# Hybrid decoder layer on one core: a third weight block loaded by halves into general buffers, and tiles at multiples of 128 bytes

## The chip, the cores and the metric

The kernel runs on one core of a Trainium2 chip. The metric is the device time of one execution in microseconds (us); less is better. Times of before are the median of three runs, and one further execution was taken with the hardware profiler on.

## What is computed

One layer with a residual stream of 256 tokens by 2048 channels. The input is normalised, multiplied by one wide matrix `w_in`, and split into the operands of two token mixers (a gated linear attention and a differential attention) and of two merge gates. Each mixer's output goes through its own 2048 by 2048 matrix, the two are merged, go through `w_out`, are normalised and added to the input.

```python
h = rmsnorm(x, pre_norm_g[l])
proj = h @ w_in[l]
(a_q, a_k, a_v, a_g, a_lr, b_q, b_k, b_v, b_g, m_a, m_b) = jnp.split(proj, offsets, axis=-1)
...
y_a = o_a @ w_branch_a[l]
...
y_b = o_b @ w_branch_b[l]
merged = jax.nn.sigmoid(m_a) * y_a + jax.nn.sigmoid(m_b) * y_b
out = merged @ w_out[l]
x = x + rmsnorm(out, post_norm_g[l])
```

## The kernel before

All weights are read once from memory, in 1 MB tiles of 128 by 2048 numbers, by DMAs that SyncE (SP in the profile) issues in a fixed order. Each tile is used as two halves of 128 by 1024. For a half, ScalarE (ACT) writes `hi`, the number rounded to the short format that the matrix unit takes at full rate (L231), and VectorE (DVE) writes `lo`, what the rounding left out (L232). TensorE (PE) then multiplies `hi` by the high and the low part of the activations and `lo` by the high part; the three products together keep the accuracy. `emit_half` prepares halves four ahead of their use (`AHEAD`), and `hi` and `lo` have three buffers each.

A matmul has two operands in on-chip memory (SBUF): a stationary one of 128 by 128, which a weight load (PEld) brings into the array, and a moving one of up to 512 columns, which streams past. Nearly every matmul here has a weight load of its own.

- In `half_tile` (L407) and `block_products` (L648) the activations are stationary and the weights move, 512 columns at a time. The activations are `xs` (the input), the pairs `oah`/`oal` and `obh`/`obl` (outputs of the two mixers), `mh`/`ml` (the merged stream), and `s4`, `r1`, `s2`, `r3` (sums of blocks of the input, from `sum_operands`).
- In `half_channel` (L427 with 512 columns, L429 with 256) the weights are stationary and `xs` moves.

The merge gate m_b is computed as two **sets**, `set0` and `set1`, by a block scheme with seven products in place of eight (`PRODUCTS`, in the order 1, 3, 5, 6, 2, 7, 4). A set's matrix is cut into four blocks, each of two tiles t = 0, 1. Blocks 1 and 4 are loaded by SP (`link`), the second block is added into the first by a DMA of GpSimd (POOL) that accumulates, and so on: the tiles `a` and `b` are changed in place from one product to the next. Product 2 uses the third block by itself (`raws[s, t]`, the tile `raw_c` in the profile), and `follow_set` then adds it into `a` on DVE (L186), a half at a time, for product 7. The steps of the two sets are interleaved with those of `others` (the last value group and the keys and queries of the first mixer), in the order that `phase_steps` writes out. In the profile this stage lies between about 81 and 277 us.

Where tiles lie is decided by pools. `const` comes first and holds tiles of odd sizes; then `wpool` (three buffers `raw` of 8 KB, three `hi`, three `lo`), then `big` (18 general buffers of 4 KB, handed out by `u`), then, for the first part of the kernel, the pool `first`, in whose place the pools `small` and `more` come later. A tile starts at a multiple of 32 bytes. With the sizes as they are, the tiles of `wpool` and `big` start 32 bytes past a multiple of 128, and those of `more` and the sums in `first` 96 bytes past one. So `xs`, `mh`, `ml`, `hi` and `lo` lie at 32, and `oah`, `oal`, `obh`, `obl`, the scores `ath`/`atl` of the first mixer and the eight tiles of the sums at 96. The 128 by 128 pieces that a matmul takes from a tile are a whole number of 512 bytes apart, so that this holds for each piece.

A new tile in a pool takes the buffer that has been out longest, and its DMA waits until the last reader of that buffer is done. All `raw` tiles and `raw_c` share the three buffers of `wpool`. SP issues its DMAs in order: one that waits for a buffer holds up those behind it.

Of the kernel before, what the change touches and what calls it, by code (L numbers as in the profile page):

```python
# [6 lines left out]
F32 = mybir.dt.float32  # L7
F32R = mybir.dt.float32r
# [3 lines left out]
ALU = mybir.AluOpType  # L12
AX = mybir.AxisListType

P = 128
# [14 lines left out]
MORE = 13  # L30
# [52 lines left out]
def hybrid_kernel(ctx: ExitStack, tc, xt, xn, preg, postg, w, w2, gkb, glag, lamv, diffg, ident_d, causal_d, lmask_d, out):  # L83
    nc = tc.nc
    pe, act, dve, pool, sp = nc.tensor, nc.scalar, nc.vector, nc.gpsimd, nc.sync

    const = ctx.enter_context(tc.tile_pool(name="const", bufs=1))
    wpool = ctx.enter_context(tc.tile_pool(name="wpool", bufs=3))
# [2 lines left out]
    psum = ctx.enter_context(tc.tile_pool(name="psum", bufs=4, space=bass.MemoryType.PSUM))  # L91

    joint = ExitStack()
    pools = [joint.enter_context(tc.tile_pool(name="first", bufs=2))]
    count = [0]

    def u(shape, name, dtype=F32):
        count[0] += 1
        return big.tile(shape, dtype, tag="u", name=f"{name}_{count[0]}")

    def u2(shape, name, dtype=F32):
        count[0] += 1
        return pools[1].tile(shape, dtype, tag="u2", name=f"{name}_{count[0]}")

    def sm(shape, name, dtype=F32, bufs=2):
        count[0] += 1
        return pools[0].tile(shape, dtype, tag=name, name=f"{name}_{count[0]}", bufs=bufs)

    def t2(shape, name):
        count[0] += 1  # L110
        return pools[0].tile(shape, F32, tag="t2", name=f"{name}_{count[0]}", bufs=6 if len(pools) == 1 else 8)

    def spill(t, name):
        count[0] += 1
# [13 lines left out]
    def f32(ap):  # L128
        return ap.bitcast(F32)
# [22 lines left out]
    raws = {}  # L152
    chain = {}

    def weights(key, r):
        a, size = at[key][r]
        return w[a : a + P * size].rearrange("(p n) -> p n", p=P), size

    def link(s, name, t):
        count[0] += 1  # L160
        c = pools[0].tile([P, 2048], F32, tag="chain", name=f"{name}_{count[0]}", bufs=4)
        sp.dma_start(c, weights(f"set{s}", {"a": 0, "b": 6}[name] + t)[0])
        chain[s, name, t] = c

    def emit_set(s, prod, t, h):
        c = slice(1024 * h, 1024 * h + 1024)
        if h == 0 and prod == 1:
            if s == 0:
                link(s, "a", t)
            link(s, "b", t)  # L170
        if h == 0 and prod == 4 and s == 0:
            link(1, "a", t)
        if h == 0 and prod == 2:
            count[0] += 1
            raws[s, t] = wpool.tile([P, 2048], F32, tag="raw", name=f"raw_c_{count[0]}")
            sp.dma_start(raws[s, t], weights(f"set{s}", 4 + t)[0])
        a, b = chain[s, "a", t], chain[s, "b", t]
        if prod == 6:
            dve.tensor_tensor(out=a[:, c], in0=a[:, c], in1=b[:, c], op=ALU.add)
        return (raws[s, t] if prod == 2 else b if prod in (3, 7) else a)[:, c]  # L180

    def follow_set(s, prod, t, h):
        c = slice(1024 * h, 1024 * h + 1024)
        a, b = chain[s, "a", t], chain[s, "b", t]
        if prod == 2:
            dve.tensor_tensor(out=a[:, c], in0=a[:, c], in1=raws[s, t][:, c], op=ALU.add)  # L186
        if h == 1 and prod in (1, 6):
            pool.dma_start(a if prod == 1 else b, weights(f"set{s}", 2 + t)[0], accum_op=ALU.add)

# [25 lines left out]
    def emit_half():  # L215
        j = emitted[0]
        emitted[0] += 1
        e = seq[j]
        joined = e[0] == "set"
        r = emit_set(*e[1:]) if joined else emit_plain(j, *e)  # L220
        n = r.shape[1]
        if e[0] == "o3" and j + 1 < len(seq):
            make = u if e[1:] == (3, 0) else u2
            hi_t, lo_t = make([P, 1024], "keep", F32R), make([P, 1024], "keep", F32R)
        else:
            hi_t = wpool.tile([P, 1024], F32R, tag="hi", name=f"hi_{j}")
            lo_t = wpool.tile([P, 1024], F32R, tag="lo", name=f"lo_{j}")
        fine = 2 if j < 2 else 1
        for i in range(fine):
            a, b = n * i // fine, n * (i + 1) // fine  # L230
            act.activation(hi_t[:, a:b], r[:, a:b], AF.Copy)  # L231
            dve.tensor_tensor(out=lo_t[:, a:b], in0=r[:, a:b], in1=f32(hi_t[:, a:b]), op=ALU.subtract)  # L232
        if joined:
            follow_set(*e[1:])
        ready[j] = (e, hi_t, lo_t)
# [28 lines left out]
    def prep_x(kt):  # L264
# [5 lines left out]
        dve.scalar_tensor_tensor(out=lo, in0=src, scalar=g, in1=f32(hi), op0=ALU.mult, op1=ALU.subtract)  # L270

    ssum = t2([P, 512], "ssum")

    def square_x(i):
        src = xraw[i // 2][:, 2 * (i % 2) : 2 * (i % 2) + 2, :].rearrange("p a t -> p (a t)")
        t = t2([P, 512], "xsq") if i else ssum
        tc.keep_in_program_order(act.activation(t, src, AF.Square))
        if i:
            dve.tensor_tensor(out=ssum, in0=ssum, in1=t, op=ALU.add)
# [22 lines left out]
    ones = const.tile([P, P], F32, name="ones")  # L302
    dve.memset(ones, 1.0)
    ones_b = t2([P, BRIDGE], "ones_b").bitcast(BF16)[:, :BRIDGE]
    dve.memset(ones_b, 1.0)
    warm = ps("bg")
# [2 lines left out]
    rstd = const.tile([P, 2], F32, name="rstd")  # L309
    half_rstd = const.tile([P, 2], F32, name="half_rstd")  # L310
    minus_half = const.tile([P, 2], F32, name="minus_half")
    rstd_bc = const.tile([P, S], F32, name="rstd_bc")
    neg_lam = const.tile([P, 1], F32, name="neg_lam")
    neg_scale = const.tile([P, 2, 2], F32, name="neg_scale")
# [132 lines left out]

    vh, vl = [None] * 4, [None] * 4
    vspill = [None] * 4
    lr = u([P, 2, P], "lr")  # L450
    pool.memset(lr, 0.0)

    ones_r = const.tile([P, P], F32R, name="ones_r")
# [80 lines left out]
    def sum_operands():  # L534
        for kt in range(KT):
            x = xraw[kt // 4][:, kt % 4, :]
            act.activation(x, x, AF.Copy, scale=preg_s[:, kt : kt + 1])
            if kt % 4 == 3:
                yield
        temps = []  # L540
        for n in range(2):
            count[0] += 1
            temps.append(pools[0].tile([P, 2, 8, P], F32, tag="chain", name=f"temp_{count[0]}", bufs=4))
        r1, s2, r3, s4 = (temps[n // 2][:, n % 2] for n in range(4))

        def part(i, j, q):
            return xraw[2 * j + q][:, :, P * i : P * i + P]

        def rows(t, q):
            return t[:, 4 * q : 4 * q + 4]  # L550

        def split(name, t):
            hi, lo = (sm([P, 8, P], f"{name}{e}", F32R, bufs=1) for e in "hl")
            act.activation(hi, t, AF.Copy)
            dve.tensor_tensor(out=lo, in0=t, in1=f32(hi), op=ALU.subtract)
            sums[name] = hi, lo

        for q in range(2):
            dve.tensor_tensor(out=rows(r1, q), in0=part(1, 1, q), in1=part(1, 0, q), op=ALU.subtract)
            dve.scalar_tensor_tensor(out=rows(s2, q), in0=rows(r1, q), scalar=-1.0, in1=part(0, 0, q), op0=ALU.mult, op1=ALU.subtract)  # L560
        yield
        for q in range(2):
            dve.scalar_tensor_tensor(out=rows(s4, q), in0=rows(s2, q), scalar=-1.0, in1=part(0, 1, q), op0=ALU.mult, op1=ALU.subtract)
        split("s4", s4)
        yield
        split("r1", r1)
        yield
        split("s2", s2)
        yield
        for q in range(2):  # L570
            dve.tensor_tensor(out=rows(r3, q), in0=part(0, 0, q), in1=part(1, 0, q), op=ALU.subtract)
        split("r3", r3)
# [8 lines left out]
    first_groups(first_joint())  # L581
    tasks.append(late())
    tasks.append(sum_operands())
    start = 2 * VG[0] - RANK
    for g in (2, 3):
# [90 lines left out]
    for gen in (sets, rest):  # L676
        assert next(gen, DONE) is DONE
    joint.close()
    pools[0] = ctx.enter_context(tc.tile_pool(name="small", bufs=2))
    pools.append(ctx.enter_context(tc.tile_pool(name="more", bufs=MORE)))  # L680
    tasks.append(forget_gate())


# [135 lines left out]
    for g in range(4):  # L819
        banks = token_major(f"ag{g}", 512, x_ops, 2)  # L820
        t = u2([P, 2, 512], "ua")
# [128 lines left out]
    def merge_gate(g, make):  # L950
        banks = token_major(f"m0{g}", 512, x_ops, 2)
        t = [make(b) for b in range(2)]
        for b in range(2):
            act.activation(t[b], banks[b], AF.Tanh, scale=half_rstd[:, b : b + 1])
        return t

    m0 = []
    for g in range(2):
        t = u([P, 2, 512], "mgate")
# [9 lines left out]
    for g in range(4):  # L969
        part.append(fetch(m0[g], "part", u) if g < 2 else u([P, 2, 512], "part"))  # L970
        banks = token_major(f"y0{g}", 512, a_ops)
        for b in range(2):
            t = part[g][:, b, :]
# [8 lines left out]
    for g in range(2, 4):  # L982
        t = merge_gate(g, lambda b: t2([P, 512], "mgate"))
# [26 lines left out]
    for g in range(4):  # L1010
        banks = token_major(f"y1{g}", 512, b_ops, 1 if g else 2, None if g else settle)
        for b in range(2):
            t = gb[g][:, b, :]
# [11 lines left out]
    for b in range(2):  # L1025
        xres.append([])
        for i in range(2):
            t = u([P, 1024], "xres")
# [47 lines left out]
    for c in range(2):  # L1076
        bank = ps("mm")
        for kt in range(KT):
            lo = 512 * (kt % 2) + 256 * c
# [66 lines left out]
```

## Time and profile before

| what | before |
|---|---|
| median of 3 runs | 1149.97 us (1147.6 to 1150.31) |
| profiled execution, whole | 1149.55 us |
| profiled execution, span from first to last instruction | 1147.7 us |
| PE busy in the span | 1127.6 us |
| DVE busy in the span | 761.0 us |
| ACT busy in the span | 640.9 us |
| granted TensorE clock, mean | 0.994 |
| bytes moved by DMA | 230.48 MB |

The profile is that of one execution. Its parts are: busy times by engine, the span in slices, DMA queues, the chain of work that ended last (followed back from the end, at each step to what released it), the costliest groups of instructions, and views by time (a timeline, windows, waits). In the chain and the timeline a row is start, length, engine, tile names, line and how many instructions were merged. Matmuls are pipelined, so that the time between two starts, and not the length of one, is what a matmul costs; in the chain a run of matmuls is merged, and its length divided by its count is that time.

### The profile page before, as it was taken

The page shows a single profiled execution, that of the slowest core. Times are in us where ns is not written, and L with a number is a line of the kernel's source. Part 1 is how long each engine was busy: PE and PEld are TensorE (multiplying, and loading weights), DVE is VectorE, ACT ScalarE, POOL GpSimd, SP SyncE. Part 2 cuts the span into 40 slices and gives each one's busy share as a digit, 9 for nine tenths or more (in the row PEclk, how much of TensorE's full clock was granted, in tenths as well). Part 3 has the DMA queues.
Part 4 walks back from the last instruction along what each step waited for, and adds up shares of the span by engine and source line. Part 5 has one row for each costly group of instructions (what it writes and reads, how often), then busy time and mean ns, then how long its engine had stood idle before and what let it go on. Part 6 is the DMA issues. An engine that isn't in the chain of part 4 may idle for free.

```text
span 1147.7 us, 14888 instructions
## 1 busy us (share of the span) xinstructions
PE 1127.6 (98%) x5642; PEld 961.2 (84%) x5642; DVE 761.0 (66%) x1088; ACT 640.9 (56%) x957; POOL 71.6 (6%) x101
## 2 busy tenths in 40 slices
PE   9999999999999999999999999999999999999996
PEld 7999788788888888888888888888888888888886
DVE  7878876777579974577567555447666765565462
ACT  7856565556756554575656444446665665444460
POOL 0110000102031010100000000000000100000000
PEclk9999999989999999999999999999999999999998
DMA  8798777755555566355455544555455565555751
GB/s 312 263 358 226 225 294 215 193 184 184 183 190 178 200 238 257 118 177 182 148 202 186 197 164 172 182 197 176 175 173 182 191 226 177 174 179 209 275 196 74
DMA packets 37783, 230.48 MB, mean 201 GB/s; under 512 B 4752, under 2 KB 6288, under 8 KB 14672
## 3 DMA queue, kind: packets, MB, share of 16 engines
q1 hardware_dynamic: 31392, 204.89, 50.6%
q0 software_dynamic: 5312, 23.33, 7.5%
q10 hardware_dynamic: 1008, 1.32, 0.3%
q8 instruction: 44, 0.72, 0.3%
q14 instruction: 27, 0.22, 0.1%
HBM read 220.08 MB, written 9.44 MB: 200 GB/s over the span
## 4 chain that ended last, share of the span: by engine, by line
PE 93%; DMA 3%; ACT 1%; DVE 1%; issue 1%; DVEq 0%; SPq 0%; POOLq 0%; POOL 0%; ACTq 0%
PE mm L407 55%; PE mm L427 10%; PE mm L648 5%; PE mm L429 5%; PE bg L427 4%; PE bg L429 2%; DMA raw_c<-in_w_dram 2%; PE bg L390 2%; PE mm L375 2%; PE mm L390 2%; PE bg L407 1%; PE bg L748 1%; DMA raw<-in_w_dram 1%; PE bg L375 1%; PE bg L859 1%
## 5 line engine op out<-in xcount | busy, mean ns | idle before, releaser
L232 DVE TENSOR_TENSOR lo<-raw,hi 128x1024 fp32r<-128x1024 f32 (+3 forms) x355 | 428.6, 1209 | 271.8 <-ACT hi L231 268.9
L231 ACT ACTIVATE hi<-raw 128x1024 fp32r<-128x1024 f32 (+3 forms) x355 | 367.2, 1036 | 354.3 <-PE mm L407 234.6
L407 PE MATMUL mm<-hi,xs 128*128 128x512 f32 (+1 forms) x1152 | 283.4, 388 | 0.0
L407 PEld LDWEIGHTS mm<-hi,xs 128*128 128x128 f32 x1152 | 213.2, 188 | 37.8
L407 PE MATMUL mm<-lo,xs 128*128 128x512 f32 (+1 forms) x576 | 151.6, 385 | 0.0
L427 PE MATMUL mm<-xs,hi 128*128 128x512 f32 x512 | 132.8, 394 | 0.0
L407 PEld LDWEIGHTS mm<-lo,xs 128*128 128x128 f32 x576 | 108.0, 188 | 20.4
L427 PEld LDWEIGHTS mm<-xs,hi 128*128 128x128 f32 x512 | 92.3, 189 | 16.1
L429 PEld LDWEIGHTS mm<-xs,lo 128*128 128x128 f32 x512 | 69.8, 190 | 5.1
L429 PE MATMUL mm<-xs,lo 128*128 128x256 f32 x512 | 71.3, 282 | 0.0
L427 PE MATMUL bg<-xs,hi 128*128 128x512 f32 x256 | 66.9, 392 | 1.2 <-ACT hi L231 1.2
L427 PEld LDWEIGHTS bg<-xs,hi 128*128 128x128 f32 x256 | 48.1, 189 | 11.8 <-ACT hi L231 2.0
L407 PE MATMUL mm<-hi,obh 128*128 128x512 f32 x128 | 51.3, 401 | 0.0
L407 PE MATMUL mm<-hi,oah 128*128 128x512 f32 x128 | 51.1, 399 | 0.0
L870 ACT ACTIVATE prob<-prob,mx,score_scale 128x128 f32<-128x128 f32 x64 | 34.3, 537 | 29.2 <-DVE mx L865 29.2
L407 PE MATMUL mm<-hi,oal 128*128 128x512 f32 x128 | 50.6, 395 | 0.0
L407 PE MATMUL mm<-hi,obl 128*128 128x512 f32 x128 | 50.4, 394 | 0.0
L231 ACT ACTIVATE hi<-a 128x1024 fp32r<-128x1024 f32 x32 | 33.6, 1059 | 28.7 <-PE bg L427 14.7
L232 DVE TENSOR_TENSOR lo<-a,hi 128x1024 fp32r<-128x1024 f32 x32 | 38.7, 1223 | 15.9 <-ACT hi L231 14.5
L429 PEld LDWEIGHTS bg<-xs,lo 128*128 128x128 f32 x256 | 35.5, 194 | 9.7 <-DVE lo L232 7.4
L429 PE MATMUL bg<-xs,lo 128*128 128x256 f32 x256 | 36.7, 287 | 6.5 <-DVE lo L232 6.5
L321 POOL TENSOR_TENSOR de<-de,neg_half 128x2 f32<-128x2 f32 x16 | 11.5, 722 | 460.0 <-DVE de L898 460.0
(279 smaller groups left out, 1565.2 us busy)
## 6 DMA issues: line engine op xcount, KB each, us to landing
raw<-in_w_dram SPq DMA_DIRECT2D x160, 1024.0 KB, 5.0
raw<-in_w_dram SPq DMA_DIRECT2D x14, 832.0 KB, 6.4
a<-in_w_dram SPq DMA_DIRECT2D x4, 1024.0 KB, 7.5
b<-in_w_dram SPq DMA_DIRECT2D x4, 1024.0 KB, 7.5
a<-in_w_dram POOLq DMA_DIRECT2D x4, 1024.0 KB, 11.1
b<-in_w_dram POOLq DMA_DIRECT2D x4, 1024.0 KB, 8.6
raw_c<-in_w_dram SPq DMA_DIRECT2D x4, 1024.0 KB, 8.6
raw<-in_w_dram SPq DMA_DIRECT2D x4, 800.0 KB, 8.1
```

Of the source, the lines that this page charges most:

```text
L231: act.activation(hi_t[:, a:b], r[:, a:b], AF.Copy)
L232: dve.tensor_tensor(out=lo_t[:, a:b], in0=r[:, a:b], in1=f32(hi_t[:, a:b]), op=ALU.subtract)
L321: pool.tensor_tensor(out=dst, in0=src, in1=neg_half[:, : src.free_size()], op=ALU.pow)
L375: i = pe.matmul(out, lhs, rhs, start=first and n == 0, stop=last and n == len(pairs) - 1)
L390: i = pe.matmul(banks[g][b][:, :n], a[part][:, P * b : P * b + P], w[:, n * g : n * g + n], start=first, stop=last)
L407: i = pe.matmul(banks[b][:, :n], a[part][:, P * b : P * b + P], w[:, n * j : n * j + n], start=first, stop=last)
L427: i = pe.matmul(o, hi[:, c], x_pair(kt), start=kt == 0, stop=kt == KT - 1)
L429: i = pe.matmul(o[:, :S], lo[:, c], x_ops(kt)[0], start=False, stop=False)
L648: i = pe.matmul(out, a[part], w[:, 512 * j : 512 * j + 512], start=first, stop=last, skip_group_check=out is x)
L748: pe.matmul(o, xk[:, P * c : P * c + P], xq.rearrange("p (b c t) -> p b c t", b=2, c=4)[:, :, c, :], start=i == 0, stop=i == 1)
L859: pe.matmul(banks[m][:, lo:up], q2[:, m, i2, t], kh[:, m, i2, :n], start=True, stop=False)
L870: act.activation(prob[m][:, lo:up], prob[m][:, lo:up], AF.Exp, scale=score_scale[:, b : b + 1], bias=mx[:, i : i + 1], accum_out=z[:, i : ...
```

## The change

Two things are changed.

First, the third block of a set is no longer loaded as two 1 MB tiles into the `raw` buffers, but as four half tiles of 512 KB, each into a general buffer of `big` (`u([P, 1024], "c")`). A half is loaded by its own DMA when its step is prepared, and `raws` is indexed by the half too.

Second, tiles are moved. A tile `margin` of 96 bytes is put into `const`, and `lr` moves there from `big`; `wpool` and `big` then start at a multiple of 128 bytes. `a`, `b`, the two `temp` tiles and the sums' parts get a pool `blocks` of their own, which starts ahead of `first`; `more` is opened ahead of `small`. Every tile that a matmul reads as its stationary operand (and every moving operand but the second half of the 400-column group) then starts at a multiple of 128. The ring `t2` of 2 KB buffers has five buffers in place of six in the first part of the kernel.

```diff
     joint = ExitStack()
+    blocks = joint.enter_context(tc.tile_pool(name="blocks", bufs=2))
     pools = [joint.enter_context(tc.tile_pool(name="first", bufs=2))]
...
-        return pools[0].tile(shape, F32, tag="t2", name=f"{name}_{count[0]}", bufs=6 if len(pools) == 1 else 8)
+        return pools[0].tile(shape, F32, tag="t2", name=f"{name}_{count[0]}", bufs=5 if len(pools) == 1 else 8)
...
-        c = pools[0].tile([P, 2048], F32, tag="chain", name=f"{name}_{count[0]}", bufs=4)
+        c = blocks.tile([P, 2048], F32, tag="chain", name=f"{name}_{count[0]}", bufs=4)
...
-        if h == 0 and prod == 2:
-            count[0] += 1
-            raws[s, t] = wpool.tile([P, 2048], F32, tag="raw", name=f"raw_c_{count[0]}")
-            sp.dma_start(raws[s, t], weights(f"set{s}", 4 + t)[0])
+        if prod == 2:
+            raws[s, t, h] = u([P, 1024], "c")
+            sp.dma_start(raws[s, t, h], weights(f"set{s}", 4 + t)[0][:, c])
...
-        return (raws[s, t] if prod == 2 else b if prod in (3, 7) else a)[:, c]
+        return raws[s, t, h] if prod == 2 else (b if prod in (3, 7) else a)[:, c]
...
-            dve.tensor_tensor(out=a[:, c], in0=a[:, c], in1=raws[s, t][:, c], op=ALU.add)
+            dve.tensor_tensor(out=a[:, c], in0=a[:, c], in1=raws[s, t, h], op=ALU.add)
...
+    const.tile([P, 24], F32, name="margin")
...
-    lr = u([P, 2, P], "lr")
+    lr = const.tile([P, 2, P], F32, name="lr")
...
-            temps.append(pools[0].tile([P, 2, 8, P], F32, tag="chain", name=f"temp_{count[0]}", bufs=4))
+            temps.append(blocks.tile([P, 2, 8, P], F32, tag="chain", name=f"temp_{count[0]}", bufs=4))
...
-            hi, lo = (sm([P, 8, P], f"{name}{e}", F32R, bufs=1) for e in "hl")
+            hi, lo = (blocks.tile([P, 8, P], F32R, tag=f"{name}{e}", name=f"{name}{e}", bufs=1) for e in "hl")
...
-    pools[0] = ctx.enter_context(tc.tile_pool(name="small", bufs=2))
-    pools.append(ctx.enter_context(tc.tile_pool(name="more", bufs=MORE)))
+    more = ctx.enter_context(tc.tile_pool(name="more", bufs=MORE))
+    pools[:] = ctx.enter_context(tc.tile_pool(name="small", bufs=2)), more
```

The change moves instructions in two places of each set, since the order on an engine is made by a scheduler that knows which buffers are free. Numbers behind the names count tiles; they are about four higher after the change for the same tile.

On SP, where set 0's third block is loaded, these rows stood before:

```order
L203 DMA raw_1140<-in_w_dram 128x2048
L203 DMA raw_1227<-in_w_dram 128x2048
L176 DMA raw_c_1239<-in_w_dram 128x2048
L176 DMA raw_c_1289<-in_w_dram 128x2048
L203 DMA raw_1313<-in_w_dram 128x2048
L203 DMA raw_1370<-in_w_dram 128x2048
L203 DMA raw_1458<-in_w_dram 128x2048
```

And these stand there after it:

```order
L176 DMA c_1243<-in_w_dram 128x1024
L203 DMA raw_1078<-in_w_dram 128x1600
L203 DMA raw_1144<-in_w_dram 128x2048
L203 DMA raw_1231<-in_w_dram 128x2048
L203 DMA raw_1319<-in_w_dram 128x2048
L203 DMA raw_1378<-in_w_dram 128x2048
L176 DMA c_1279<-in_w_dram 128x1024
L203 DMA raw_1466<-in_w_dram 128x2048
L176 DMA c_1295<-in_w_dram 128x1024
L176 DMA c_1331<-in_w_dram 128x1024
```

The first half of tile t = 0 has moved ahead by three tiles; the `raw` tile that came behind the two `raw_c` has taken the first one's place; the second half of t = 0 stands behind one more `raw` tile, and both halves of t = 1 behind two more (`raw_1378`, `raw_1466`). None of the `c` tiles waits for a `raw` buffer itself, but each stands behind one that does.

On DVE, the rows from the first add of the third block (L186) on stood before as follows; `lo_1230` and `lo_1266` are the two halves of the plain tile `raw_1227`:

```order
L186 TENSOR_TENSOR a_808<-a_808,raw_c_1239 128x1024
L232 TENSOR_TENSOR lo_1194<-a_867,hi_1193 128x1024
L232 TENSOR_TENSOR lo_1207<-a_867,hi_1206 128x1024
L186 TENSOR_TENSOR a_808<-a_808,raw_c_1239 128x1024
L186 TENSOR_TENSOR a_867<-a_867,raw_c_1289 128x1024
L232 TENSOR_TENSOR lo_1230<-raw_1227,hi_1229 128x1024
L232 TENSOR_TENSOR lo_1242<-raw_c_1239,hi_1241 128x1024
L614 TENSOR_TENSOR k_1203<-bg_1204,k_1203 128x2x128
L232 TENSOR_TENSOR lo_1266<-raw_1227,hi_1265 128x1024
```

After the change they are:

```order
L186 TENSOR_TENSOR a_812<-a_812,c_1243 128x1024
L232 TENSOR_TENSOR lo_1198<-a_871,hi_1197 128x1024
L232 TENSOR_TENSOR lo_1211<-a_871,hi_1210 128x1024
L232 TENSOR_TENSOR lo_1234<-raw_1231,hi_1233 128x1024
L232 TENSOR_TENSOR lo_1246<-c_1243,hi_1245 128x1024
L615 TENSOR_TENSOR k_1207<-bg_1208,k_1207 128x2x128
L232 TENSOR_TENSOR lo_1270<-raw_1231,hi_1269 128x1024
L617 TENSOR_TENSOR k_1207<-k_1207,rstd_bc 128x2x128
L659 TENSOR_TENSOR gr_917<-mm_915,p_92_1170 128x512
L186 TENSOR_TENSOR a_812<-a_812,c_1279 128x1024
L232 TENSOR_TENSOR lo_1282<-c_1279,hi_1281 128x1024
```

The adds of the second and third half no longer stand ahead of `lo` of the plain tile: each stands directly ahead of the `lo` of its own half. Set 1 changes in the same way on DVE; on SP its first two halves stand directly behind `raw_2020`, and the other two behind three `raw` tiles more.

## The prediction, made before the changed kernel ran

> **What bounds the kernel now.** I read the page first: span, busy times and the chain of work that ended last.
>
> ```profile
> span 1147.7 us, 14888 instructions
> PE 1127.6 (98%) x5642; PEld 961.2 (84%) x5642; DVE 761.0 (66%) x1088; ACT 640.9 (56%) x957; POOL 71.6 (6%) x101
> PE 93%; DMA 3%; ACT 1%; DVE 1%; issue 1%; DVEq 0%; SPq 0%; POOLq 0%; POOL 0%; ACTq 0%
> ...
> raw<-in_w_dram SPq DMA_DIRECT2D x160, 1024.0 KB, 5.0
> ...
> raw_c<-in_w_dram SPq DMA_DIRECT2D x4, 1024.0 KB, 8.6
> ```
>
> 93% of the chain is TensorE. So only two things can shorten the run: a shorter time from one matmul to the next, or a stall of PE that goes. The change touches one of each.
>
> For the first I read the chain in order of time. A row is start, length, what ran, and how many matmuls were merged, so length by count is the cost of one.
>
> ```profile
> 150.78 2.80 PE mm L648 x12
> ...
> 622.48 16.80 PE mm L407 x72
> ...
> 724.16 38.12 PE mm L407 x168
> ...
> 973.79 16.80 PE mm L407 x72
> ...
> 1053.76 61.72 PE mm L407 x272
> ```
>
> At 724 us `xs` is stationary and at 1053 us `mh`/`ml`; all of them lie 32 bytes past a multiple of 128: 38.12 / 168 = 226.9 ns and 61.72 / 272 = 226.9 ns. At 622 us it is `oah`/`oal` and at 973 us `obh`/`obl`, at 96 bytes past: 16.80 / 72 = 233.3 ns both times. At 150 us it is the sum `r3`, also at 96: 2.80 / 12 = 233.3 ns. The moving operand has 512 columns and the same place in all five. So the place of the stationary operand and the step of 6.4 ns go together. Is it the clock, or what the other engines do meanwhile? A table by windows says no to the clock (1.00 in each of these; the columns are window, length, busy time with its count on PE, PEld, DVE, ACT and POOL, granted clock, DMA share and GB/s):
>
> ```profile
> 640.00:650.00 10.00, 10.00 (x45) 8.10 (x44) 7.89 (x20) 5.20 (x11) 0.00 (x0) 1.00 0.49 186
> 740.00:750.00 10.00, 10.00 (x46) 8.28 (x45) 4.77 (x4) 5.05 (x6) 0.00 (x0) 1.00 0.60 210
> 1060.00:1070.00 10.00, 10.00 (x46) 8.27 (x45) 4.21 (x4) 4.24 (x4) 0.00 (x0) 1.00 1.03 421
> ```
>
> The third has a far fuller DMA than the second and the same 226.9 ns. I take placement as the cause.
>
> For the second I read the waits, and then the timeline around the two longest.
>
> ```profile
> DVE a L186 <- DMA raw_c<-in_w_dram: 10.5, 3, 6.2
> ...
> PE bg L429 <- DVE lo L232: 6.5, 2, 4.3
> ```
>
> ```profile
> 128.25 1.23 DVE L186 TENSOR_TENSOR a<-a,raw_c 128x1024 f32<-128x1024 f32 x1 [3.24 <-DMA raw_c<-in_w_dram]
> 129.39 1.22 DVE L232 TENSOR_TENSOR lo<-raw,hi 128x1024 fp32r<-128x1024 f32 x1
> ...
> 126.49 1.99 PE L427 MATMUL bg<-xs,hi 128*128 128x512 f32 x8
> 130.66 1.21 PE L429 MATMUL bg<-xs,lo 128*128 128x256 f32 x8 [2.19 <-DVE lo L232]
> ...
> 139.38 0.96 PE L427 MATMUL bg<-xs,hi 128*128 128x512 f32 x3 [0.61 <-ACT hi L231]
> ...
> 228.70 1.23 DVE L186 TENSOR_TENSOR a<-a,raw_c 128x1024 f32<-128x1024 f32 x1 [6.20 <-DMA raw_c<-in_w_dram]
> ...
> 231.12 2.07 PE L429 MATMUL bg<-xs,lo 128*128 128x256 f32 x8 [4.33 <-DVE lo L232]
> ```
>
> In both sets DVE stands at the add of the second `raw_c` tile until that tile has landed. Behind the add, on the same engine, waits the `lo` of a plain tile, and PE waits for that. The load is late because it has to wait for a `raw` buffer:
>
> ```profile
> 119.35 8.80 DMA raw_c<-in_w_dram
> ...
> 217.32 11.29 DMA raw_c<-in_w_dram
> ```
>
> After the longer stall the clock fell too:
>
> ```profile
> 232.00:240.00 8.00, 8.00 (x35) 6.81 (x35) 6.88 (x11) 3.56 (x6) 0.00 (x0) 0.77 0.63 220
> ...
> 142.45 1.39 PE mm L648 x6
> ...
> 231.12 2.07 PE bg L429 x8
> 233.19 2.56 PE mm L648 x6
> ...
> 237.38 0.95 PE bg L429 x8
> ```
>
> Eight L429 took 2.07 us there and 0.95 later, six L648 2.56 against 1.39 elsewhere: 1.12 + 1.17 = 2.3 us lost.
>
> **The sum, part by part.** It is made against the profiled execution's own 1149.55 us (span 1147.7 and 1.85 around it), 0.4 below the median of 1149.97.
>
> *Placement.* The groups by form give the counts: six groups of 128 at L407 (`oah`, `oal` and `obh`, `obl`, with `hi` and `lo`), and twelve of 16 at L648 for the sums; here the first and the last of each.
>
> ```profile
> L407 PE MATMUL mm<-hi,obh 128*128 128x512 f32 x128 | 51.3, 401 | 0.0
> ...
> L407 PE MATMUL mm<-lo,obh 128*128 128x512 f32 x128 | 35.0, 395 | 0.0
> ...
> L648 PE MATMUL mm<-hi,r3l 128*128 128x512 f32 x16 | 6.4, 398 | 0.0
> ...
> L648 PE MATMUL mm<-lo,s4h 128*128 128x512 f32 x16 | 5.0, 395 | 0.0
> ```
>
> 768 x 6.4 ns = 4.9 us. 192 x 6.4 = 1.2 us at most; these run in sixes between other shapes, and after a change of shape even operands at 32 do not start at 226.9 (six L648 on `xs` took 1.39 us, 232 ns each), so I take 1.0, with 0.3 as the low end. The 36 matmuls of the first mixer's scores (L375) add 0.2. Together 6.1 us, between 5.4 and 6.3.
>
> What 0 does in place of 32 for the other tiles, no row shows, as no stationary operand lies at 0 today. The nearest rows, 32 and 96, differ by 6.4 ns over 64 bytes. Carried on in a line, 32 bytes less give 3.2 ns less; turned around, 6.4 more. I take nothing. The rows at 32 have both operands at the same place modulo 128, as has everything after the change, and those at 96 have not: if the distance between the two operands counts, 0 and 0 cost what 32 and 32 do. Both ends come back among the rivals.
>
> *The third block.* What goes: 2.19 + 0.61 in set 0, 4.33 + 2.3 in set 1, 9.4 us together. What is late next: the third half (tile t = 1, first half) is issued behind a plain tile that needs the buffer of the tile whose `lo` of the second half must come first. In set 0, by the times above and without the stall: PE starts the first plain half at 126.49; a plain half costs 1.81 + 0.95 = 2.76, a half of a set 1.39.
>
> ```profile
> 762.28 1.81 PE mm L427 x8
> 764.10 0.95 PE mm L429 x8
> ...
> L186 DVE TENSOR_TENSOR a<-a,raw_c x8: 1216/1218/1226, 120.4 to 235.7; 128x1024 f32<-128x1024 f32 x8
> L231 ACT ACTIVATE hi<-raw_c x8: 1037/1053/1063, 124.9 to 239.8; 128x1024 fp32r<-128x1024 f32 x8
> L232 DVE TENSOR_TENSOR lo<-raw_c,hi x8: 1215/1218/1220, 130.5 to 241.1; 128x1024 fp32r<-128x1024 f32 x8
> L176 SPq DMA_DIRECT2D raw_c<-in_w_dram x4: 327/328/328, 111.9 to 217.3; - x4
> ```
>
> So PE wants the third half's `hi` at 126.49 + 2.76 + 1.39 + 2.76 + 1.39 = 134.8, and its `lo` 0.9 later, at 135.7. The plain tile's second `lo` ends at about 126.5 + 1.05 + 1.22 = 128.8 (its `hi` buffer comes free as PE starts at 126.5). Then the next plain tile is issued and lands 5.0 us later, and the half behind it after 512 KB more, 1.25 us at the 421 GB/s of the fullest window: 135.0. The add and `lo` take 2 x 1.22: 137.5. PE waits 1.8 us, in each set. If the plain tile takes the 8.6 us that `raw_c` took, it is 5.4 us a set; if the DMA runs ahead, nothing. I take 1.8, nearest to the median of 160 plain tiles: 3.6 us stay of 9.4, **5.8 us go**, with the ends at -1.4 and 9.4. A wait of 1.8 us is below the 2.19 us that left the clock at 1.00, so nothing is charged for the clock.
>
> The second half is issued at about 119.7, right behind a plain tile in the place of the second `raw_c`, which landed at 119.35 + 8.80 = 128.15. With 1.25 us more it is there at 129.4, and add and `lo` end at 131.9; PE wants that `lo` at 134.3. Behind the waiting adds DVE holds only `lo` of the same or later steps, no longer one that PE needs first.
>
> *Edits costed at nothing.* Four more DMA issues of 0.33 us on SP, which waits for DVE far more than that; the ring `t2` with one buffer less, whose tiles ACT and DVE use while PE has work in hand (one wait in the open costs about an ACT instruction, 1 us); `lr`, `margin` and the pools' order, which move no work. Ends 0 and 1 us.
>
> Sum: 6.1 + 5.8 = 11.9; 1149.55 - 11.9 = 1137.65, say **1137.6 us**. The likeliest case's own range is 1133 to 1145.
>
> **Rivals.**
>
> *Placement at 0 is cheaper for every matmul.* A fixed part stands in every gap: 512 columns cost 1.81 / 8 = 226 ns and 256 cost 0.95 / 8 = 119 ns (L427 and L429 above), 0.42 ns a column, and 226 - 512 x 0.42 leaves about 12 ns. At 96 bytes it was 6.4 more, so that part does depend on the place. Counted in the program, 5,204 matmuls have 256 to 512 columns. By the line above each would lose 3.2 ns, 17 us: 1121. If the fixed part went whole, 5,204 x 12 = 62 us: 1076. Against it: it has no row, and the equal distances at 32 may be the cheap case already. TensorE would still be the bound, with DVE at 66%. The Trainium skill, "TensorE: Matmul & The Clock Gate", section "Back-to-back issue gap", counts 518 cycles for 512 columns, some 216 ns; by that figure the sum would be near this rival's lower end, and no run here shows it. 20%.
>
> *Placement does nothing*, and 226.9 against 233.3 comes from something else that differs between these stages; only the loads pay: 1149.55 - 5.8 = 1143.7. For it: DVE was busier at 640 than at 740 us. Against it: the 233.3 come back to the digit at 622, 973 and 150 us in three different stages. The Trainium skill, same page, section "Step-by-step: what each phase is for", gives the array two independent read ports, so that a weight load takes no bandwidth from a running matmul; by that rule this rival's time holds. The five rows speak against reading it so strictly. 9%.
>
> *The loads win nothing*, since each `c` half stands behind a plain tile that waits for a buffer: at the 8.6 us landing the stalls are as long as now, and only placement pays: 1143.5. 5%.
>
> *Slower: 0 is the dear place.* If the place itself counts and 0 is like 96, the 2,788 matmuls of 512 columns now at 32 go up by 6.4 ns, 17.8 us, and those at 96 gain nothing: 1149.55 + 17.8 - 5.8 = 1161.6. It decides from 5.8 us / 2,788 = 2.1 ns a matmul on, that is from 229 ns. 7%.
>
> **How the numbers follow.** The forecast has 59%. The range reaches up to 1146.5, which takes in the two partial cases, and down to 1104, which takes in somewhat over half of the first rival; left out are the rest of it and the slower case, some 16%. What a measurement of this kernel tells from no change is 0.3%, that is 3.4 us: the border to faster is 1146.5. Faster: 59 + 20 + 5 + 3 = 87%, with half of the two partial cases and their spread; same: 6%; slower: 7%.
>
> **What would show each step.** Placement: runs of L407 on `oah` and `obh` at 226.9 ns in the chain, as on `xs` and `mh`; the first rival would show all of them lower, the slower one all near 233. Third block: no wait of DVE at L186 ahead of a plain `lo`; in its place a wait of PE under 2 us for the third half in each set, and the clock at 1.00 around 230 us. The forecast is wrong if the gap on `xs` moves by over 1 ns, or if PE waits over 4 us in a set.

## The result, and the profile after

| | before | after |
|---|---|---|
| median | 1149.83 us, 4 runs (1147.60 to 1150.31) | 1143.39 us, 4 runs (1141.73 to 1143.92) |
| ratio after to before | | 0.9945, 95% interval 0.9928 to 0.9963 |
| profiled execution | 1149.55 us, span 1147.7 | 1143.88 us, span 1142.1 |
| PE busy in the span | 1127.6 us | 1123.8 us |

The change is faster by 6.4 us, where 11.9 were forecast. From the page of after, the lines that answer to those of before:

```profile
span 1142.1 us, 14888 instructions
...
PE 1123.8 (98%) x5642; PEld 963.4 (84%) x5642; DVE 761.3 (67%) x1088; ACT 640.6 (56%) x957; POOL 72.2 (6%) x101
...
PE 94%; DMA 2%; ACT 1%; DVE 1%; issue 1%; SPq 0%; DVEq 0%; POOLq 0%; POOL 0%; ACTq 0%
...
c<-in_w_dram SPq DMA_DIRECT2D x8, 512.0 KB, 7.9
```

TensorE is the bound as before, and the DMA's share of the chain has hardly fallen (3% to 2%). Of the change's two parts one looks as forecast. These are the rows of the chain of work that answer to those of before (start, length, what ran, matmuls merged): `xs`, then `obh`/`obl`, then `mh`/`ml`.

```profile
720.92 38.11 PE mm L408 x168
...
970.18 16.36 PE mm L408 x72
...
1048.38 61.70 PE mm L408 x272
```

38.11 / 168 and 61.70 / 272 are 226.8 ns, against 226.9 on these operands before. 16.36 / 72 is 227.2, where 233.3 stood. So 0 is neither cheaper nor dearer than 32, and what lay at 96 came down.

The third block does not look as forecast. The same chain around the two stalls:

```profile
128.19 0.33 SPq L203
128.60 6.23 DMA c<-in_w_dram
134.92 1.07 ACT hi L231
136.03 1.83 PE mm L649 x4
...
226.27 0.33 SPq L203
226.65 8.55 DMA c<-in_w_dram
235.28 1.06 ACT hi L231
236.39 2.07 PE mm L649 x4
```

And the timeline of PE at these two places, with its wait in brackets, and the windows behind them (the clock is the third number from the end):

```profile
136.03 1.83 PE L649 MATMUL mm<-hi,xs 128*128 128x512 f32 x4 [1.78 <-ACT hi L231]
...
236.39 2.07 PE L649 MATMUL mm<-hi,xs 128*128 128x512 f32 x4 [4.06 <-ACT hi L231]
```

```profile
136.00:139.00 3.00, 2.97 (x8) 2.33 (x9) 3.00 (x4) 2.93 (x3) 0.00 (x0) 0.56 0.00 0
...
236.00:241.00 5.00, 4.61 (x11) 3.64 (x12) 5.00 (x6) 3.29 (x4) 0.00 (x0) 0.50 0.00 0
```

In set 0 the third half landed 6.23 us after its issue, at 134.83; 135.0 was forecast. PE waited 1.78 us; 1.8 was forecast. But a stretch at half speed followed (granted clock 0.50), which was not charged. In set 1 the third half took 8.55 us to land, PE waited 4.06 us, and half speed followed for longer. The old wait of PE for the `lo` of a plain tile is gone, as forecast; a wait for the third half's `hi`, of about the same size, stands in its place.

To compare runs I add up, from the starts of the matmuls in the trace, what each gap has over the usual gap of its shape, where that is over 150 ns. For the stalls of the two sets, half speed included, that gives 3.1 + 6.0 = 9.1 us before and 3.5 + 7.0 = 10.5 us after. So the half tiles seemed to have cost 1.4 us in place of paying 5.8. Did they?

### The profile page after: what moved, and what is told of

It is laid out like the page before. It is cut to its first block, busy times and chain, and to the rows that moved or that the text cites. A ratio compares the mean times of both kernels' runs of the same rounds, so it can differ in the third digit from the quotient of the medians.

```text
span 1142.1 us, 14888 instructions
## 1 busy us (share of the span) xinstructions
PE 1123.8 (98%) x5642; PEld 963.4 (84%) x5642; DVE 761.3 (67%) x1088; ACT 640.6 (56%) x957; POOL 72.2 (6%) x101
## 4 chain that ended last, share of the span: by engine, by line
PE 94%; DMA 2%; ACT 1%; DVE 1%; issue 1%; SPq 0%; DVEq 0%; POOLq 0%; POOL 0%; ACTq 0%
PE mm L408 55%; PE mm L428 10%; PE mm L649 6%; PE mm L430 5%; PE bg L428 4%; PE bg L430 2%; PE bg L391 2%; PE mm L376 2%; PE bg L408 2%; PE mm L391 2%; DMA c<-in_w_dram 1%; PE bg L749 1%; ACT hi L231 1%; PE bg L376 1%; DVE lo L232 1%
## 5 line engine op out<-in xcount | busy, mean ns | idle before, releaser
L232 DVE TENSOR_TENSOR lo<-a,hi 128x1024 fp32r<-128x1024 f32 x32 | 38.9, 1223 | 15.5 <-ACT hi L231 15.3
L408 PE MATMUL mm<-hi,mh 128*128 128x512 f32 x96 | 37.5, 390 | 0.0
L408 PE MATMUL mm<-hi,ml 128*128 128x512 f32 x96 | 37.4, 390 | 0.0
```

What stands on the lines that cost most here:

```text
L408: i = pe.matmul(banks[b][:, :n], a[part][:, P * b : P * b + P], w[:, n * j : n * j + n], start=first, stop=last)
```

## The experiments

Times are medians; "saved" is the median of before of the same call less that of the kernel (1149.83 us for the change, 1150.07 for e1 to e4, 1150.38 for e5 to e8, 1150.39 in one run for e9 and e10). The stalls are counted as above, from the profiled execution of each.

| run | time, us | saved, us | ratio to before (95% interval) | stalls set 0 + set 1, us |
|---|---|---|---|---|
| the change | 1143.39 | 6.4 | 0.9945 (0.9928 to 0.9963) | 3.5 + 7.0 |
| e1: placement alone | 1144.72 | 5.4 | 0.9962 (0.9948 to 0.9976) | 3.8 + 6.8 |
| e2: half tiles alone | 1142.98 | 7.1 | 0.9943 (0.9931 to 0.9955) | 1.6 + 1.6 |
| e3: change, halves a product earlier | 1133.51 | 16.6 | 0.9858 (0.9846 to 0.9871) | 0 + 0 |
| e4: change, `w2` later | 1138.91 | 11.2 | 0.9903 (0.9888 to 0.9917) | 2.2 + 1.8 |
| e5: change, `lr` put back | 1138.63 | 11.8 | 0.9896 (0.9883 to 0.9909) | 3.5 + 1.8 |
| e6: half tiles and `lr`, no placement | 1147.85 | 2.5 | 0.9987 (0.9973 to 1.0001) | 2.0 + 5.5 |
| e7: all operands at 96 | 1142.19 | 8.2 | 0.9928 (0.9914 to 0.9941) | 3.8 + 6.8 |
| e8: weight ring 64 bytes off | 1159.03 | -8.7 | 1.0070 (1.0056 to 1.0084) | 4.0 + 5.3 |
| e9: weight ring 32 bytes off | 1161.23 | -10.8 | one run | 1.6 + 5.2 |
| e10: weight ring 96 bytes off | 1158.60 | -8.2 | one run | 2.0 + 6.2 |

### e1: placement alone

```diff
-        if prod == 2:
-            raws[s, t, h] = u([P, 1024], "c")
-            sp.dma_start(raws[s, t, h], weights(f"set{s}", 4 + t)[0][:, c])
+        if h == 0 and prod == 2:
+            count[0] += 1
+            raws[s, t] = wpool.tile([P, 2048], F32, tag="raw", name=f"raw_c_{count[0]}")
+            sp.dma_start(raws[s, t], weights(f"set{s}", 4 + t)[0])
...
```

The two lines that read these tiles go back with it.

> The changed kernel with the third block loaded as before (two 1 MB raw_c tiles in the weight ring), so that placement stands alone. Theory 'placement paid, the half tiles did not': the gaps between matmuls are those of the changed kernel (6.4 us less than before in sum) and the stalls those of the kernel before (9.4 us instead of about 10.5), so 1142 to 1144 us, at or just below the changed kernel. Rival 'both paid': placement is worth less than 6 us and the half tiles pay part of it, so 1145 to 1148 us.

1144.72 us, just over the upper end of the first theory. By the interval of the ratio it is 1144.1 to 1147.3 us, which leaves the first theory's range and lies mostly in the rival's 1145 to 1148. The gaps are those of the changed kernel, and the stalls those of before and somewhat more. So placement pays about 5.4 us (2.8 to 6.0 by the interval).

### e2: the half tiles alone

The kernel before, with the lines of e1's diff the other way round and nothing else.

> The kernel before with nothing changed but the third block: eight half tiles in general buffers, every operand at its old place. Theory 'the half tiles did not pay': within 2 us of before, 1149 to 1151.5 us, with a wait of PE for hi of the third half in each set, and a lower clock behind it. Rival 'both paid': 1144 to 1147 us.

1142.98 us: **the theory fell, and its rival by a little too**. Alone, the half tiles pay 7.1 us (5.2 to 7.9 by the interval). PE waits for the third half in each set as forecast, and no half speed follows:

```profile
135.97 1.20 PE L647 MATMUL mm<-hi,xs 128*128 128x512 f32 x4 [1.47 <-ACT hi L230]
...
232.75 1.19 PE L647 MATMUL mm<-hi,xs 128*128 128x512 f32 x4 [1.47 <-ACT hi L230]
```

So each part alone pays about what the forecast gave it (5.4 and 7.1 for 6.1 and 5.8, 12.5 for 11.9 in sum), and both together pay 6.4. Some 6 us are lost where they meet. The set that changed most is set 1: 1.6 us of stalls here, 7.0 there.

### e4: the load of `w2` out of the way

What runs on the DMA beside the third half in set 1? GpSimd's rows in the timeline of the changed kernel show a transfer that the prediction never named: `w2_raw` (`w_raw` in the profile), the second matrix of the forget gate. Its buffer is cleared on POOL and then filled by four DMAs of 64 KB.

```profile
224.84 0.96 POOL L469 MEMSET w_raw<- 128x1024 f32 x1 [9.58 <-DVE lo L232]
226.09 1.97 POOL L471 DMA_DIRECT2D w_raw<-in_w_dram  x4 [0.30 <-POOL w_raw L469]
```

It goes out at 226.09, and the third half at 226.65. In e4 its buffer comes from the pool that opens only after the sets:

```diff
-        w2_raw, w2_s = u([P, 1024], "w2_raw"), u([P, 1024], "w2_s", F32R)
+        w2_raw, w2_s = u2([P, 1024], "w2_raw"), u([P, 1024], "w2_s", F32R)
```

> The changed kernel with w2_raw taken from the pool that opens after the sets, so that the four w2 loads no longer run beside the third half in set 1. Theory 'the longer wait of set 1 is the w2 load beside it': c lands 6 to 6.5 us after issue instead of 8.55, PE waits 1.8 to 2.2 us instead of 4.1, 1139.5 to 1141.5 us. Rival 'set 1 is late for another reason (VectorE behind by then)': the landing stays over 8 us and the time within 1 us of the changed kernel.

1138.91 us, 0.6 better than the lower end. The third half of set 1 now lands in 6.15 us, by the chain of e4:

```profile
226.95 6.15 DMA c<-in_w_dram
...
234.29 1.20 PE mm L649 x4
```

So `w2` beside it was the reason for the longer wait.

### e5 and e6: why it stands there

Why does `w2` go out at 226.09 in the changed kernel, and not in e2? Its clear waits 9.58 us for a `lo` on DVE. It needs the general buffer that has been out longest, and that is now one of the `c` halves. Which one, the ring decides, and the change turns the ring by one: `lr` no longer takes a general buffer. e5 undoes this one line.

```diff
-    lr = const.tile([P, 2, P], F32, name="lr")
+    lr = u([P, 2, P], "lr")
```

> The changed kernel with one line undone: lr is a general buffer again, which turns the ring of general buffers by one, so that w2_raw gets the buffer of the second c half instead of the first. Theory 'the two parts spoil each other through that ring': the w2 loads start some 2.4 us later in set 1, c lands under 6.5 us after issue, PE waits 1.5 to 2 us there instead of 4.1 with no half speed behind it, 1137 to 1139.5 us. Rival 'lr is nothing': within 1.5 us of the changed kernel's 1143.4.

1138.63 us, as the theory had it, 4.8 better than the changed kernel (5.3 by the saved column). First the rows of the changed kernel for the `lo` of the first two `c` halves of set 1:

```profile
223.56 1.22 DVE L232 TENSOR_TENSOR lo<-c,hi 128x1024 fp32r<-128x1024 f32 x1
...
227.10 1.22 DVE L232 TENSOR_TENSOR lo<-c,hi 128x1024 fp32r<-128x1024 f32 x1
```

Its clear of `w2_raw` started at 224.84, as the first of them ended (223.56 + 1.22 = 224.78). Now e5, its DVE, POOL and chain:

```profile
226.70 1.22 DVE L232 TENSOR_TENSOR lo<-c,hi 128x1024 fp32r<-128x1024 f32 x1
```

```profile
227.97 0.95 POOL L469 MEMSET w_raw<- 128x1024 f32 x1 [13.11 <-DVE lo L232]
229.22 1.97 POOL L471 DMA_DIRECT2D w_raw<-in_w_dram  x4 [0.30 <-POOL w_raw L469]
```

```profile
226.25 6.12 DMA c<-in_w_dram
...
233.57 1.21 PE mm L649 x4
```

Here the clear waits for the second (226.70 + 1.22 = 227.92), `w2` goes out at 229.22, 3 us behind the third half in place of 0.6 us ahead of it, and the third half lands in 6.12 us.

e6 asks the same from the other side: the half tiles alone (e2), with `lr` moved as the only addition.

```diff
-    lr = u([P, 2, P], "lr")
+    lr = const.tile([P, 2, P], F32, name="lr")
```

> The kernel before with the half tiles and with lr among the constants, and every operand at its old place. By the same theory this gives back what the half tiles paid alone: w2 beside the third half, PE waits about 4 us in set 1 with half speed behind it, 1147 to 1149.5 us. Rival 'lr is nothing': 1142.4 to 1144 us, as the half tiles alone.

1147.85 us: the line that moves no instruction of its own costs 4.9 us against e2 (4.6 by the saved column). The chains of e2 and of e6 show the same tile at almost the same issue (e2's `w2` goes out at 228.50, e6's at 224.90):

```profile
225.53 6.03 DMA c<-in_w_dram
...
232.75 1.19 PE mm L647 x4
```

```profile
225.46 8.54 DMA c<-in_w_dram
...
235.19 2.07 PE mm L647 x4
```

That settles where the two parts meet. The kernel before seems to have had the same collision in set 1, for another reason: its rows, which could have been read before the prediction, show `w2` going out with the second `raw_c` tile.

```profile
217.31 1.97 POOL L470 DMA_DIRECT2D w_raw<-in_w_dram  x4 [0.30 <-POOL w_raw L468]
```

`raw_c` was issued at 217.32 and landed in 11.29 us, 2.5 more than in set 0. No run took `w2` away from the kernel before, so for it this is a reading of rows.

### e3: the halves a product earlier

The stalls that stay in e4 and e5 come from SP's order: the third half is issued right behind a plain tile that waits for its buffer. In e3 each half is asked for at product 6, the one before product 2 in the order of the set.

```diff
-        if prod == 2:
+        if prod == 6:
             raws[s, t, h] = u([P, 1024], "c")
```

> The changed kernel with each c half asked for one product earlier, so that all four stand ahead of the plain tiles on SP's queue. Theory 'late because it is issued behind a plain tile that waits for its buffer': both waits of PE for the third half (1.8 and 4.1 us) and the half-speed stretches behind them go, up to 10 us in all, so 1133 to 1136 us. Rival 'the DMA is full there': the same megabytes come in another order, a plain tile is late in place of c, and 1140 to 1144 us remain.

1133.51 us, and both waits are gone. In the view of the waits, the row of the changed kernel and then the only one that e3 has for PE in the sets:

```profile
PE mm L649 <- ACT hi L231: 5.8, 2, 4.1
```

```profile
PE bg L428 <- ACT hi L231: 0.6, 2, 0.4
```

9.9 us better than the changed kernel, 16.6 better than before: this version beats both. The DMA had room for the same bytes at an earlier time. `w2` still waits for a `c` half there, but no `c` half is under way any more when it goes out.

### e7 to e10: place or distance

After the change stationary and moving operand start at the same place modulo 128, which was one of two readings of the 6.4 ns; the other was the place of the stationary operand. e7 puts both at 96, e8 moves the ring of `raw`, `hi`, `lo` by 64 bytes and leaves the rest at 0.

```diff
-    const.tile([P, 24], F32, name="margin")
+    const.tile([P, 48], F32, name="margin")
```

```diff
+    ctx.enter_context(tc.tile_pool(name="near", bufs=1)).tile([P, 16], F32, name="near")
     wpool = ctx.enter_context(tc.tile_pool(name="wpool", bufs=3))
+    ctx.enter_context(tc.tile_pool(name="far", bufs=1)).tile([P, 16], F32, name="far")
```

> The changed kernel with 96 bytes more of margin, so that stationary and moving operands all lie at 96 modulo 128. Theory 'the distance between the two operands counts': the gap of 512 columns stays at 226.9 ns everywhere and the time at 1142 to 1145 us. Rival 'the place of the stationary operand counts and 96 is dear': 233.3 ns on all 3,784 matmuls of 512 columns, 24 us more, 1166 to 1169 us.

> The changed kernel with the weight ring (hi, lo, raw) moved by 64 bytes and everything else left at multiples of 128. L408 then has its stationary operand at 0 and the moving one at 64, L428 and L430 the other way round. Theory 'the distance counts': about 233.3 ns on L408 (2,600 of 512 columns, 17 us) and on L428 (768, 5 us), 1162 to 1167 us. Rival 'the place of the stationary operand counts': L408 stays at 226.9 ns and only L428 can move, 1143 to 1149 us.

e7 took 1142.19 us, e8 1159.03 (below the range of its theory, and far above that of its rival). The chains of e7 and of e8, `oah`/`oal` and `mh`/`ml`:

```profile
621.23 16.37 PE mm L408 x72
...
1048.10 61.67 PE mm L408 x272
```

```profile
627.47 16.80 PE mm L410 x72
...
1061.49 63.47 PE mm L410 x272
```

At 96 and 96 the gap is 226.7 to 227.4 ns; at 0 and 64 it is 233.3 for both kinds of operand, the ones that were never dear before included. **The distance between the two operands counts, not the place.** The Trainium skill, "TensorE: Matmul & The Clock Gate", section "Step-by-step: what each phase is for", has two independent read ports, so that a weight load takes nothing from a running matmul; these four rows, the same matmuls with the same loads, differ by 6.0 and 6.6 ns, and only the places of the operands are different.

The full step shows where the activations are stationary. In `half_channel`, where the weights are, the 512-column gap rose far less: from 229.3 ns in the changed kernel to 231.0 in e8, in the mean over its matmuls.

Over all 512-column gaps under 300 ns between matmuls of one line, by their starts in the trace, the mean is 227.95 ns in the changed kernel (3,450 gaps) and 232.75 in e8 (3,453); the 256-column ones of `half_channel` went the other way, from 118.9 to 117.1 (672). That makes 16.5 - 1.2 = 15.3 us, and 15.6 were measured. The 22 us of the expectation took the steady 6.4 ns for every gap, those of `half_channel` included.

e9 and e10 move the ring by 32 and by 96 bytes, with 8 and 24 numbers in `near`, 24 and 8 in `far`.

> The changed kernel with the weight ring moved by 32 bytes instead of 64, all else at multiples of 128. Theory 'any distance costs': a median gap near 233 ns for 512 columns. Theory 'only a distance of 64 costs': 227 ns. Theory 'it grows with the distance': about 230 ns.

> The changed kernel with the weight ring moved by 96 bytes. Theory 'any distance costs': 233 ns for 512 columns. Theory 'only a distance of 64 costs': 227 ns. Theory 'it grows with the distance': 230 ns if it counts around the ring of 128 bytes, as at 32, or about 236 ns if it does not.

The row of `mh`/`ml` in the chain of e9, and then of e10:

```profile
1063.71 63.73 PE mm L410 x272
```

```profile
1061.33 63.46 PE mm L410 x272
```

234.3 and 233.3 ns: every distance tried cost it, 32 as much as 64 and 96, which bears out the first theory of three. Each of the two is a single run.

## Why the prediction was right and where it was wrong

- **The sign and the range** were right: 1143.39 lies between 1104 and 1146.5, and in the likeliest case's own 1133 to 1145. The size was wrong: 11.9 us forecast, 6.4 measured. The time is that of the rival "the loads win nothing", 1143.5, but not for its reason: it gave plain tiles that land in 8.6 us, and the loads alone win 7.1 us (e2).
- **Placement**, 6.1 us forecast: e1 saved 5.4. From the starts in the trace, the summed gaps of the 768 matmuls on `oah`, `oal`, `obh`, `obl` fell by 4.3 us (4.9 forecast), those of the sums by 0.7 (1.0), the scores by 0.2 (0.2). The 6.4 ns hold for the steady gap; gaps at the head of a run fell by less. "I take nothing" for 0 against 32 was right, and the reason behind it, the equal distance, is now shown (e7, e8). Both rivals on 0 fell: `xs` stayed at 226.8 ns.
- **The third block**, 5.8 us forecast: about right for the half tiles alone (e2), with waits of 1.47 us in each set for 1.8, and stalls of 3.2 us in place of 9.1. In set 0 of the changed kernel the landing came out at 134.83 for 135.0. That the wait was 1.78 for 1.8 is in part luck: the prediction let PE stand from 135.7 to 137.5 for the `lo`, while PE came at 134.25 and stood for the `hi`, which was ready at 135.99.
- **The step that failed** stands among the edits costed at nothing: "`lr`, `margin` and the pools' order, which move no work. Ends 0 and 1 us." `lr` moves no work of its own, but it turned the ring of general buffers, which decides when the `w2` load goes out. It put `w2` ahead of the third half of set 1, which then landed in 8.55 us in place of 6.12. That cost 4.8 us (e5) to 4.9 us (e6), most of the miss of 5.8. The prediction also took the landing of set 0 for both sets; the 2.5 us between 8.80 and 11.29 in its own rows were not explained, and the POOL rows of before would have done it.
- **The clock**: "A wait of 1.8 us is below the 2.19 us that left the clock at 1.00, so nothing is charged for the clock" was wrong. In the changed kernel 1.78 us was followed by half speed: eight matmuls of 427 ns for 227, 1.6 us. The place of the wait in time mattered too (last section).
- **Nothing for `t2` and the added issues** on SP: no run took these apart. In e3 no stall is left in the sets, so they can cost little.

## What to carry to other kernels

A tile that leaves a ring of shared buffers, or enters one, changes which buffer every later tile waits for: read off what the next takers of that ring wait for, DMAs on other queues above all, before an edit of placement is costed at nothing. When two landings of the same transfer differ by microseconds, look in the timeline at all queues in that stretch; here the reason stood there. And load pieces that stand on an in-order queue behind a tile waiting for its buffer a step earlier; here that was worth 9.9 us more than the whole change had given.

## What the runs showed of the hardware

- With the activations stationary, a weight load for each matmul and 512 columns, the gap from start to start was 226.7 to 227.4 ns with both operands at the same place modulo 128 bytes (0, 32 and 96 tried) and 233.3 to 234.3 ns at distances of 32, 64 and 96. With the weights stationary (`half_channel`) a distance of 64 cost 1.7 ns at 512 columns, and 256 columns were cheaper with it, 117.1 ns against 118.9. Why, no run shows.
- Four DMAs of 64 KB beside 1.5 MB made a half tile land 2.4 to 2.5 us later (6.12 to 8.55, 6.03 to 8.54). 256 KB at the 421 GB/s of the fullest window would be 0.6 us, so more than their bytes is lost. From 231 to 234 us SP's queue moved 0.55 MB in the changed kernel, and POOL's 0.20; in e4 SP's alone moved 0.90. In e5 the four went out at 229.22, but up to the landing of the half at 232.37 the trace has no packet of POOL's queue. Why the packets of the one slow the other stays open.
- The length of a wait alone did not say whether half speed follows. After 1.78 us it did in set 0 of the changed kernel and of e5, where the clock was 0.56 and 0.50; after 1.47 (e2), 2.01 (e4) and 2.19 us (before) it did not. The windows of e5 (set 0) and of e4 (set 0):

```profile
137.00:139.50 2.50, 2.50 (x7) 2.00 (x6) 2.50 (x3) 1.39 (x2) 0.00 (x0) 0.50 0.00 0
```

```profile
137.80:141.00 3.20, 3.17 (x14) 2.50 (x15) 3.20 (x4) 2.83 (x3) 0.00 (x0) 1.00 0.00 0
```

  The Trainium skill, "TensorE: Matmul & The Clock Gate", section "HAM oscillation — how this bites in real kernels", puts the limit at gaps of about 3.4 us. The trace does not agree: 1.78 us was enough twice.

  The clock records of the traces show what goes with it. In each of the twelve traces the granted clock changes only on a grid of steps of 3.41 us: in the changed kernel it fell at 136.34, rose at 139.75, fell at 235.32 and rose at 242.15, that is 1, 28 and 2 steps apart. Two steps of the changed kernel and two of e4, each cut along its own grid:

```profile
132.93:136.34 3.41, 1.63 (x7) 1.05 (x6) 2.33 (x4) 2.20 (x4) 0.00 (x0) 1.00 0.66 245
136.34:139.75 3.41, 3.41 (x9) 2.63 (x8) 3.41 (x4) 2.59 (x3) 0.00 (x0) 0.50 0.00 0
```

```profile
134.00:137.41 3.41, 1.82 (x9) 1.18 (x7) 2.21 (x4) 2.33 (x4) 0.00 (x0) 1.00 0.82 305
137.41:140.82 3.41, 2.99 (x13) 2.36 (x14) 3.41 (x4) 3.22 (x4) 0.00 (x0) 1.00 0.00 0
```

  The 1.78 us of the changed kernel lie in one step, and the next ran at half speed. The 2.01 us of e4 lie across an edge, 1.58 before it and 0.43 behind, and the clock stayed. All 22 waits of over 1 us in the sets, two in each trace but that of e3, go the same way: of the steps that ran at full clock, each that held 1.78 us or more of the wait was followed by one at half speed, and none that held 1.72 us (e8, set 1) or less. Half speed then lasted one step or two. This is read from the traces that were there; no run was made to move a wait across an edge.
